# Loads of decay rows and pooling weights placed sooner, and branch gates with two buffers stored from ScalarE's queue

## The chip, the cores and the metric

One core of a Trainium2 chip runs the whole kernel. The metric is the device time in microseconds of one execution; the time given for a kernel is the median of its runs.

## The reference

One layer of a hybrid backbone over 512 latent tokens and 256 context tokens, model width 1024, all in fp32. It is a half-step SwiGLU feed-forward (inner width 2816), then token mixing, then a second half-step feed-forward and a final norm, all modulated by a condition (adaLN). The change lies in the mixing, of which this is the core:

```python
px = ux @ w_mix_in
pc = uc @ w_mix_in[:, :AB_END]
lat_in = gdn_inputs(px[..., :AB_END], conv_w, a_log, dt_bias)   # q, k, v, beta, g
ctx_in = gdn_inputs(pc[..., :AB_END], conv_w, a_log, dt_bias)
ox, oc = bidir_gdn(lat_in, ctx_in)
mix_x = merge_branches(px, pool_grid(px[..., GATE_END:POOL_END]), ox, ...)
x = x + mx[5] * mix_x
```

`gdn_inputs` makes q, k, v of 8 heads by a short convolution, and from four small columns per head a step size beta and a decay g. `bidir_gdn` runs a gated delta rule over chunks in both directions; it needs the running sums of g (`cum`) and the factors exp(cum_i - cum_j) of each chunk. `pool_grid` takes window means minus the token in 4 groups of 128 channels, and a linear map `pool_w` (128 x 128 in each group) follows. `merge_branches` computes `sigmoid(gate_pool) * (y_pool @ w_pool_proj) + sigmoid(gate_gdn) * (y_gdn @ w_gdn_proj)` and projects it with `w_mix_out`.

## The kernel before

Every product of two fp32 matrices is made of three matmuls: each operand is cast to fp32r (the high half, by ScalarE) and the rest is subtracted (the low half, by VectorE or GpSimd). `split_act` (lines 187 to 189) does this for an activation; `weights` (107 to 112) loads a slice of a weight matrix into the tile stg by SP's queue and makes whi and wlo of it; `job` (122 to 134) runs the matmuls at line 132.

The order of the instructions on an engine is not the order of the program text. A planner goes over the traced program and places an instruction on its engine when by its plan the inputs are there and the output tile has room; of several that could go, the earlier traced goes first. On the chip each engine, and each queue of transfers, then runs its list in that order. Tiles live in pools, and a pool lies on the bytes of pools that were closed before it; with a number of buffers (`bufs`) the tiles of one tag share so many homes. `tc.keep_in_program_order(i)` pins an instruction on its engine's list behind the instruction of that engine that was traced just ahead of it; it adds order and no wait.

Around the change the program does this:

- Decay stage (pool gp, lines 625 to 685). From the small columns come beta (639), nega (609), a sigmoid (650), Ln (652), g (660), the running sums by matmuls with the triangular matrices tri (loaded at 629, used at 665), and cumd, the sums of all heads as rows, stored to DRAM at 685. `head(0)` follows: the projections and convolutions of the first head's k, q and v.
- Pooling stage (pool pb, lines 688 to 731). pw (pool_w) is loaded at 693 and split. Twice, a half of the input weights, ws (1024 x 256, 1 MB, loaded at 700), is cast into wh and wl and multiplied at line 708 with the tokens. Then four groups of window sums, the product with pw, and the store of y into y_dram (731). `head(1)` follows.
- Heads (pool mp, from line 734, which begins with the small loads eye at 740 and first at 742). Each head has three generators. `front(h)` turns k and q by TensorE, copies k to kt on ScalarE (765), and prepares norms. `invert(h)` loads two tiles crow of 384 KB at 808 (the head's row sums of one direction, the same on all partitions; tag row, three buffers), makes of them arg (Abs on ScalarE, six times for each, 817; one Exp, 819), and inverts the chunk matrices. `scan(h)` is the recurrence over the chunks. `gate(h)` makes the head's output gate.
- Branch gates (`branch_gates`, 1028 to 1036): 16 jobs of 128 columns, each copied from PSUM to the tile bgate on ScalarE (1032; one buffer) and stored by SP's queue to bg_dram (1033).

The order of these parts is written out by hand: the loop over k runs scan(k), invert(k+1) and front(k+2) interleaved, then a later head, a gate, and so many branch gates as SHARE says for this k.

```python
    ORDER = "sfifsisiissiis"
    SHARE = (3, 2, 0, 0, 0, 0, 0, 0, 6, 5)
    for k in range(-2, H):
        stages = {c: g(i) for c, g, i in (("s", scan, k), ("f", front, k + 2), ("i", invert, k + 1)) if 0 <= i < H}
```

- Merge (pools mg and yp). The pooled rows y_dram come back into yg (tag yg, two buffers, loaded at 1078), and are split into yphi and yplo; then for each of 8 column blocks the gate is loaded, its sigmoid taken (1084), and `job` multiplies with w_pool_proj. The heads' outputs, yg_dram, pass through the same tag yg (1089), and gates and products with w_gdn_proj follow (1095 to 1100).

Of the kernel before, what the change touches and what calls it, by code (L numbers as in the profile page):

```python
# [8 lines left out]
F32 = mybir.dt.float32  # L9
F32R = mybir.dt.float32r  # L10
AF = mybir.ActivationFunctionType
ALU = mybir.AluOpType
# [5 lines left out]
KT = 8  # L18
LAT = 512
# [22 lines left out]
def layer_kernel(ctx, tc, a, out):  # L42
    nc = tc.nc
    act, dve, pool, pe, sp = nc.scalar, nc.vector, nc.gpsimd, nc.tensor, nc.sync
# [142 lines left out]
    def split_act(src, hi, lo):  # L187
        act.copy(out=hi, in_=src)  # L188
        dve.tensor_tensor(out=lo, in0=src, in1=hi, op=ALU.subtract)  # L189
# [193 lines left out]
    for k in range(KT):  # L383
        for p in BOTH:
            o, m = PARTS[p]
# [5 lines left out]
    with tc.tile_pool(name="pl", bufs=1, reuse_waits="tile") as pl:  # L391
# [5 lines left out]
        t = {}  # L397
# [3 lines left out]
        for n in range(KT + AHEAD):  # L401
            if n < KT:
                k = PAIRED[n]
# [185 lines left out]
    def head(h):  # L589

        for c0, tl, parts, store, tag, bufs in ((D, 8, BOTH, kf, "kf", 4), (0, 0, ONLY, qf, "qf", 4), (2 * D, 16, BOTH, vf, "vf", 2)):
            store[h] = pj.tile([128, T if len(parts) == 2 else LAT], F32, tag=tag, name=tag, bufs=bufs)
            if h == 0 and c0 == D:
                conv_silu(None, tl, parts, store[h], res_k)
            else:
                conv_silu(weights(w_mix, 0, KT, c0 + 128 * h, EH), tl + h, parts, store[h])
# [25 lines left out]
    bwst = sm.tile([128, 6, 8, 2], F32, name="bwst")  # L622
    ncumc = sm.tile([128, 96], F32, name="ncumc")
    etot = sm.tile([128, 96], F32, name="etot")
    with tc.tile_pool(name="gp", bufs=1, reuse_waits="tile") as gp:
        cumc = gp.tile([128, 96], F32, name="cumc")
        wst = gp.tile([128, 96], F32, name="wst")
# [60 lines left out]
    with tc.tile_pool(name="pb", bufs=1, reuse_waits="tile") as pb:  # L688

        phi = pb.tile([128, 4, 512], F32R, name="phi")  # L690
        plo = pb.tile([128, 4, 512], F32R, name="plo")
        pw = pb.tile([128, 4, 128], F32, name="pw")
        sp.dma_start(out=pw, in_=a["pool_w"].rearrange("(g p) m -> p g m", p=128))
        pwh = pb.tile([128, 4, 128], F32R, name="pwh")
        pwl = pb.tile([128, 4, 128], F32R, name="pwl")
        split_act(pw, pwh, pwl)
        for g2 in range(2):
            wh = pb.tile([128, KT, 256], F32R, tag="wh", name="wh", bufs=1)
            ws = pb.tile([128, KT, 256], F32, tag="ws", name="ws", bufs=2)
            sp.dma_start(out=ws, in_=w_mix[:, 4128 + 256 * g2:4384 + 256 * g2].rearrange("(k p) m -> p k m", p=128))  # L700
            wl = pb.tile([128, KT, 256], F32R, tag="wl", name="wl", bufs=1)
            split_act(ws, wh, wl)
            for t in range(4):
                r = bank("a")
                n = 0
                for k in range(KT):
                    for hh, ww in ((hhi, wh), (hlo, wh), (hhi, wl)):
                        pe.matmul(r[:, :256], lhsT=hh[:, k, t * 128:(t + 1) * 128], rhs=ww[:, k],  # L708
                                  start=n == 0, stop=n == 3 * KT - 1)
                        n += 1  # L710
                split_act(r[:, :256], phi[:, t, g2 * 256:g2 * 256 + 256], plo[:, t, g2 * 256:g2 * 256 + 256])
        for g in range(4):
# [16 lines left out]
            y = pb.tile([128, LAT], F32, tag="df", name="df", bufs=2)  # L729
            act.activation(out=y, in_=pr["lat"], func=AF.Copy, scale=vec[:, 0, R_PS + g:R_PS + g + 1])  # L730
            sp.dma_start(out=y_dram[g], in_=y)
    head(1)
    mp_cm = tc.tile_pool(name="mp", bufs=1, reuse_waits="tile")
    mp = mp_cm.__enter__()
# [8 lines left out]
    powers = mp.tile([128, 10], F32, name="powers")  # L743
    pool.memset(powers[:, 0:6], 0.5)
    pool.memset(powers[:, 6:10], -0.5)
    st = {}

    def g4(shape, name):
        return mp.tile(shape, F32, tag="g4", name=name, bufs=3)
# [6 lines left out]

    def front(h):

        kt = mp.tile([128, 6, 128], F32, tag="kt", name="kt", bufs=3)
        ss = mp.tile([128, 10], F32, tag="ss", name="ss", bufs=2)  # L760
        for c0, n in ((0, 4), (4, 2)):
# [32 lines left out]
        for c0, n in ((0, 4), (4, 2)):  # L794
            b = bank("a")
            for c in range(n):
                pe.transpose(b[:, c * 128:(c + 1) * 128], vf[h][:, (c0 + c) * 128:(c0 + c + 1) * 128], ident)
            dve.tensor_tensor(out=vt[:, c0:c0 + n], in0=b[:, :n * 128].rearrange("p (c x) -> p c x", x=128),
                              in1=bc(rr[:, c0:c0 + n].unsqueeze(2), [128, n, 128]), op=ALU.mult)
        st[h] = [kt, vt, rr, bs, nbs, w2]  # L800

    def invert(h):

        bs, nbs = st[h][3:5]
        crow = []
        for d in range(2):
            t = mp.tile([128, 6, 128], F32, tag="row", name="crow", bufs=3)
            sp.dma_start(out=t, in_=cum_rows[d, h].partition_broadcast(128))
            crow.append(t)

        L = mp.tile([128, 12, 128], F32, tag="L", name="L", bufs=2)
        aqk = mp.tile([128, 8, 128], F32, tag="aqk", name="aqk", bufs=2)
# [213 lines left out]
    def branch_gates():  # L1026
        jobs = []
        for m in range(2 * KT):
            def one(m=m):
                r = job(weights(w_mix, 0, KT, 4640 + 128 * m, EG), u_hi, u_lo, range(KT), ONLY)  # L1030
                t = mp.tile([128, LAT], F32, tag="bgate", name="bgate", bufs=1)
                act.copy(out=t, in_=r["lat"])
                sp.dma_start(out=bg_dram[m], in_=t)
            jobs.append(one)
        return jobs

# [29 lines left out]
    def m2(name, bufs=2):  # L1066
        return mg.tile([128, LAT], F32, tag=name, name=name, bufs=bufs)

    zhi, zlo = hhi[:, :, 0:LAT], hlo[:, :, 0:LAT]
    with tc.tile_pool(name="yp", bufs=1, reuse_waits="tile") as yp:  # L1070
# [3 lines left out]
        yplo = yp.tile([128, 4, LAT], F32R, name="yplo")  # L1074
        pooled = yp.tile([128, KT, LAT], F32, name="pooled")
        for g in range(4):
            t = m2("yg", 2)
            sp.dma_start(out=t, in_=y_dram[g])
            split_act(t, yphi[:, g], yplo[:, g])
        for m in range(0, KT, 2):  # L1080
            for e in range(2):
                gp_ = m2("gp")
# [2 lines left out]
                y = job(weights(a["w_pool_proj"], 0, 4, 128 * (m + e)), lambda k: yphi[:, k], lambda k: yplo[:, k], range(4), ONLY)["lat"]  # L1085
                dve.tensor_tensor(out=pooled[:, m + e], in0=gp_, in1=y, op=ALU.mult)
        for h in range(H):
            t = m2("yg", 2)
            sp.dma_start(out=t, in_=yg_dram[h])
            split_act(t, yghi[:, h], yglo[:, h])  # L1090
        sp.dma_start(out=xl, in_=x_dram)
# [176 lines left out]
```

## Time and profile before

| what | value |
|---|---|
| median of 3 runs | 1752.39 us |
| lowest and highest run | 1749.08 and 1753.36 us |
| the profiled execution, own time | 1756.71 us |
| the profiled execution, span | 1755.0 us |
| mean granted TensorE clock, share of full speed | 0.982 |
| TensorE busy | 1653.5 us, 94% of the span |
| ScalarE busy | 842.6 us, 48% |

The span runs from the first to the last instruction that the profiler recorded; the own time is the device time of that same execution. PE is TensorE's matmuls, PEld its weight loads, DVE VectorE, ACT ScalarE, POOL GpSimd, SP the engine whose queue issues nearly all transfers (SPq). In a wait, the tile or line behind the arrow is what ended the idle time. The granted clock is a share of full speed.

### The profile page before, as it was taken

How to read it: one execution, taken by the hardware profiler on the slowest of the kernel's cores; microseconds unless marked ns; L12 is line 12 of the kernel's file. 1: busy time of each engine (PE TensorE's matmuls, PEld its weight loads, DVE VectorE, ACT ScalarE, POOL GpSimd, SP SyncE). 2: the span in 40 equal slices, each digit the busy share in tenths (PEclk: the TensorE clock that was granted, in tenths of full speed). 3: DMA queues.
4: the chain of work that ended last, by engine and by line, in shares of the span. 5: the costliest groups of instructions: out<-in, count | busy, mean ns of one | idle time of the engine just before them, and what ended most of it. 6: DMA issues, size and time to landing. Idle time of an engine off the chain costs nothing.

```text
span 1755.0 us, 31315 instructions
## 1 busy us (share of the span) xinstructions
PE 1653.5 (94%) x12220; PEld 1423.9 (81%) x12220; DVE 1119.0 (64%) x2254; ACT 842.6 (48%) x1851; POOL 390.8 (22%) x493
## 2 busy tenths in 40 slices
PE   6899999999999999889999999999998999999996
PEld 4889898989999778777878788787786788888885
DVE  5778888798888886375678767774555533333333
ACT  5443343434444364667677767665443322222233
POOL 2243444444454121123323331100000000000000
PEclk9999999999999999989999999999999999999998
DMA  9355536361221325532112212224654232333321
GB/s 273 112 155 151 156 96 182 103 189 65 78 67 56 108 82 187 138 100 67 44 52 65 60 45 53 56 61 154 214 158 116 69 98 88 94 96 96 93 64 48
DMA packets 282696, 183.82 MB, mean 105 GB/s; under 512 B 7008, under 2 KB 269877, under 8 KB 282421
## 3 DMA queue, kind: packets, MB, share of 16 engines
q1 hardware_dynamic: 282112, 181.65, 35.6%
q8 instruction: 96, 1.57, 0.4%
q14 instruction: 51, 0.42, 0.1%
q10 hardware_dynamic: 437, 0.18, 0.1%
HBM read 170.22 MB, written 11.58 MB: 104 GB/s over the span
## 4 chain that ended last, share of the span: by engine, by line
PE 71%; DVE 14%; ACT 5%; DMA 5%; POOL 2%; issue 2%; SPq 0%; ACTq 0%; POOLq 0%; DVEq 0%
PE b L132 22%; PE b L345 9%; PE a L132 6%; PE g L132 6%; PE a L345 5%; PE g L345 5%; DVE cv L583 2%; PE b L279 2%; PE a L279 1%; PE g L279 1%; PE a L708 1%; ACT din L848 1%; DVE wlo L120 1%; DMA bg_dram<-bgate 1%; PE b L150 1%
## 5 line engine op out<-in xcount | busy, mean ns | idle before, releaser
L188 ACT CAST fhi<-fst 128x512 fp32r<-128x512 f32 (+1 forms) x136 | 77.7, 605 | 249.6 <-PE b L132 85.6
L132 PE MATMUL b<-hhi,whi 128*128 128x512 f32 (+1 forms) x528 | 187.6, 384 | 0.0
L132 PE MATMUL b<-hlo,whi 128*128 128x512 f32 (+1 forms) x528 | 187.5, 383 | 0.0
L132 PE MATMUL b<-hhi,wlo 128*128 128x512 f32 (+1 forms) x528 | 186.9, 384 | 0.0
L179 POOL TENSOR_TENSOR rs<-rs,mhalf 128x4 f32<-128x4 f32 (+2 forms) x13 | 13.6, 1045 | 665.3 <-DVE rs L177 649.7
L189 DVE TENSOR_TENSOR flo<-fst,fhi 128x512 fp32r<-128x512 f32 (+1 forms) x136 | 87.3, 671 | 92.6 <-ACT fhi L188 92.4
L119 ACT CAST whi<-stg 128x512 fp32r<-128x512 f32 x146 | 89.4, 620 | 91.6 <-PE b L132 59.9
L119 ACT CAST whi<-qst 128x512 fp32r<-128x512 f32 (+1 forms) x160 | 81.6, 512 | 106.5 <-PE b L345 43.2
L119 ACT CAST whi<-qs 128x512 fp32r<-128x512 f32 (+1 forms) x120 | 59.5, 512 | 115.2 <-POOL qs L309 76.2
L583 DVE SCALAR_TENSOR_TENSOR cv<-raw,vec,cv 128x772 f32<-128x772 f32 (+1 forms) x96 | 101.6, 1058 | 11.6 <-ACT cv L581 8.3
L120 DVE TENSOR_TENSOR wlo<-qst,whi 128x512 fp32r<-128x512 f32 (+1 forms) x160 | 100.7, 639 | 10.1 <-ACT whi L119 10.0
L132 PEld LDWEIGHTS b<-hlo,whi 128*128 128x128 f32 x528 | 94.0, 190 | 14.8
L132 PEld LDWEIGHTS b<-hhi,whi 128*128 128x128 f32 x528 | 94.0, 190 | 14.8
L132 PEld LDWEIGHTS b<-hhi,wlo 128*128 128x128 f32 x528 | 93.3, 190 | 14.8
L308 POOL TENSOR_TENSOR qs<-qst 128x512 f32<-128x512 f32 (+1 forms) x40 | 46.4, 1161 | 247.2 <-DMA qst<-in_ffn_w_in_dram 76.6
L120 POOL TENSOR_TENSOR wlo<-stg,whi 128x512 fp32r<-128x512 f32 x46 | 65.4, 1430 | 90.6 <-ACT whi L119 70.6
L120 DVE TENSOR_TENSOR wlo<-stg,whi 128x512 fp32r<-128x512 f32 x100 | 68.2, 686 | 22.1 <-ACT whi L119 20.2
L188 ACT CAST ahi<-q 128x384 fp32r<-128x384 f32 x74 | 37.5, 512 | 75.4 <-DVE q L257 35.6
L120 DVE TENSOR_TENSOR wlo<-qs,whi 128x512 fp32r<-128x512 f32 (+1 forms) x80 | 49.0, 613 | 32.6 <-ACT whi L119 32.6
L132 PE MATMUL b<-xlo,fhi 128*128 128x512 f32 x160 | 63.4, 396 | 0.0
L132 PE MATMUL b<-xhi,flo 128*128 128x512 f32 x160 | 63.4, 396 | 0.0
L132 PE MATMUL b<-xhi,fhi 128*128 128x512 f32 x160 | 63.4, 396 | 0.0
(512 smaller groups left out, 4909.8 us busy)
## 6 DMA issues: line engine op xcount, KB each, us to landing
stg<-in_w_ada_dram SPq DMA_DIRECT2D x56, 512.0 KB, 4.0
stg<-in_w_mix_in_dram SPq DMA_DIRECT2D x49, 512.0 KB, 3.7
fst<-in_ffn_w_in_dram SPq DMA_DIRECT2D x44, 512.0 KB, 3.6
qst<-in_ffn_w_in_dram SPq DMA_DIRECT2D x40, 512.0 KB, 3.4
qst<-in_ffn_w_out_dram SPq DMA_DIRECT2D x40, 256.0 KB, 2.6
adx<-in_w_ada_dram SPq DMA_DIRECT2D x16, 512.0 KB, 6.4
fst<-in_ffn_w_out_dram SPq DMA_DIRECT2D x16, 512.0 KB, 3.9
crow<-cumd SPq DMA_DIRECT2D x16, 384.0 KB, 7.8
```

Source lines behind the costliest of these rows:

```text
L119: (first.copy if first is act else first.tensor_copy)(out=hi[:, :n], in_=w)
L120: second.tensor_tensor(out=lo[:, :n], in0=w, in1=hi[:, :n], op=ALU.subtract)
L132: pe.matmul(res[p][:, :m], lhsT=ww(i), rhs=hh(k)[:, o:o + m], start=(i == 0 and j == 0), stop=(i == n - 1 and j == 2))
L150: pe.matmul(b[32 * j:32 * j + 32, e * 128:(e + 1) * 128], lhsT=sc[:, k, :], rhs=stg[:, k, :], start=(i == 0), stop=(i == 1))
L188: act.copy(out=hi, in_=src)
L189: dve.tensor_tensor(out=lo, in0=src, in1=hi, op=ALU.subtract)
L279: pe.matmul(x, lhsT=ww(k), rhs=rhs(j, part, k), start=n + e == 0, stop=n + e == len(ks) + 1)
L308: pool.tensor_tensor(out=s1, in0=a21, in1=a22, op=ALU.add)
L345: pe.matmul(o, lhsT=ww[:, k], rhs=rhs(j, part, k), start=first and k + i == 0, stop=k + i == nh + 1, skip_group_check=not first)
L583: dve.scalar_tensor_tensor(out=cv[:, :n], in0=raw[:, t:t + n], scalar=tap[t], in1=cv[:, :n], op0=ALU.mult, op1=ALU.add)
L708: pe.matmul(r[:, :256], lhsT=hh[:, k, t * 128:(t + 1) * 128], rhs=ww[:, k], start=n == 0, stop=n == 3 * KT - 1)
L848: act.copy(out=din[o:o + 32, :, 0:12].rearrange("p f u -> p u f"), in_=L[o:o + 32, :, o:o + 32])
```

## The change

Four edits. A pool pw is opened ahead of the decay stage's pool; it holds both ws (homes of their own), pw, pwh and pwl, and their loads and the split of pw are traced there. The two crow loads move from `invert(h)` to the start of `front(h)`, with four buffers in place of three. bgate gets two buffers, and its store is issued by ScalarE's queue. In the merge the tag yg gets four buffers, and the casts yphi are pinned in program order; yplo isn't.

```diff
--- before.py
+++ after.py
@@ -622,6 +622,16 @@
     bwst = sm.tile([128, 6, 8, 2], F32, name="bwst")
     ncumc = sm.tile([128, 96], F32, name="ncumc")
     etot = sm.tile([128, 96], F32, name="etot")
+    pw_cm = tc.tile_pool(name="pw", bufs=1, reuse_waits="tile")
+    pwp = pw_cm.__enter__()
+    pool_w = [pwp.tile([128, KT, 256], F32, tag="ws", name="ws", bufs=2) for _ in range(2)]
+    for g2 in range(2):
+        sp.dma_start(out=pool_w[g2], in_=w_mix[:, 4128 + 256 * g2:4384 + 256 * g2].rearrange("(k p) m -> p k m", p=128))
+    pw = pwp.tile([128, 4, 128], F32, name="pw")
+    sp.dma_start(out=pw, in_=a["pool_w"].rearrange("(g p) m -> p g m", p=128))
+    pwh = pwp.tile([128, 4, 128], F32R, name="pwh")
+    pwl = pwp.tile([128, 4, 128], F32R, name="pwl")
+    split_act(pw, pwh, pwl)
     with tc.tile_pool(name="gp", bufs=1, reuse_waits="tile") as gp:
         cumc = gp.tile([128, 96], F32, name="cumc")
         wst = gp.tile([128, 96], F32, name="wst")
@@ -689,15 +699,9 @@
 
         phi = pb.tile([128, 4, 512], F32R, name="phi")
         plo = pb.tile([128, 4, 512], F32R, name="plo")
-        pw = pb.tile([128, 4, 128], F32, name="pw")
-        sp.dma_start(out=pw, in_=a["pool_w"].rearrange("(g p) m -> p g m", p=128))
-        pwh = pb.tile([128, 4, 128], F32R, name="pwh")
-        pwl = pb.tile([128, 4, 128], F32R, name="pwl")
-        split_act(pw, pwh, pwl)
         for g2 in range(2):
             wh = pb.tile([128, KT, 256], F32R, tag="wh", name="wh", bufs=1)
-            ws = pb.tile([128, KT, 256], F32, tag="ws", name="ws", bufs=2)
-            sp.dma_start(out=ws, in_=w_mix[:, 4128 + 256 * g2:4384 + 256 * g2].rearrange("(k p) m -> p k m", p=128))
+            ws = pool_w[g2]
             wl = pb.tile([128, KT, 256], F32R, tag="wl", name="wl", bufs=1)
             split_act(ws, wh, wl)
             for t in range(4):
@@ -729,6 +733,7 @@
             y = pb.tile([128, LAT], F32, tag="df", name="df", bufs=2)
             act.activation(out=y, in_=pr["lat"], func=AF.Copy, scale=vec[:, 0, R_PS + g:R_PS + g + 1])
             sp.dma_start(out=y_dram[g], in_=y)
+    pw_cm.__exit__(None, None, None)
     head(1)
     mp_cm = tc.tile_pool(name="mp", bufs=1, reuse_waits="tile")
     mp = mp_cm.__enter__()
@@ -743,7 +748,7 @@
     powers = mp.tile([128, 10], F32, name="powers")
     pool.memset(powers[:, 0:6], 0.5)
     pool.memset(powers[:, 6:10], -0.5)
-    st = {}
+    st, rows_of = {}, {}
 
     def g4(shape, name):
         return mp.tile(shape, F32, tag="g4", name=name, bufs=3)
@@ -756,6 +761,11 @@
 
     def front(h):
 
+        crow = []
+        for d in range(2):
+            t = mp.tile([128, 6, 128], F32, tag="row", name="crow", bufs=4)
+            sp.dma_start(out=t, in_=cum_rows[d, h].partition_broadcast(128))
+            crow.append(t)
         kt = mp.tile([128, 6, 128], F32, tag="kt", name="kt", bufs=3)
         ss = mp.tile([128, 10], F32, tag="ss", name="ss", bufs=2)
         for c0, n in ((0, 4), (4, 2)):
@@ -798,15 +808,12 @@
             dve.tensor_tensor(out=vt[:, c0:c0 + n], in0=b[:, :n * 128].rearrange("p (c x) -> p c x", x=128),
                               in1=bc(rr[:, c0:c0 + n].unsqueeze(2), [128, n, 128]), op=ALU.mult)
         st[h] = [kt, vt, rr, bs, nbs, w2]
+        rows_of[h] = crow
 
     def invert(h):
 
         bs, nbs = st[h][3:5]
-        crow = []
-        for d in range(2):
-            t = mp.tile([128, 6, 128], F32, tag="row", name="crow", bufs=3)
-            sp.dma_start(out=t, in_=cum_rows[d, h].partition_broadcast(128))
-            crow.append(t)
+        crow = rows_of.pop(h)
 
         L = mp.tile([128, 12, 128], F32, tag="L", name="L", bufs=2)
         aqk = mp.tile([128, 8, 128], F32, tag="aqk", name="aqk", bufs=2)
@@ -1028,9 +1035,9 @@
         for m in range(2 * KT):
             def one(m=m):
                 r = job(weights(w_mix, 0, KT, 4640 + 128 * m, EG), u_hi, u_lo, range(KT), ONLY)
-                t = mp.tile([128, LAT], F32, tag="bgate", name="bgate", bufs=1)
+                t = mp.tile([128, LAT], F32, tag="bgate", name="bgate", bufs=2)
                 act.copy(out=t, in_=r["lat"])
-                sp.dma_start(out=bg_dram[m], in_=t)
+                act.dma_start(out=bg_dram[m], in_=t)
             jobs.append(one)
         return jobs
 
@@ -1074,9 +1081,10 @@
         yplo = yp.tile([128, 4, LAT], F32R, name="yplo")
         pooled = yp.tile([128, KT, LAT], F32, name="pooled")
         for g in range(4):
-            t = m2("yg", 2)
+            t = m2("yg", 4)
             sp.dma_start(out=t, in_=y_dram[g])
-            split_act(t, yphi[:, g], yplo[:, g])
+            tc.keep_in_program_order(act.copy(out=yphi[:, g], in_=t))
+            dve.tensor_tensor(out=yplo[:, g], in0=t, in1=yphi[:, g], op=ALU.subtract)
         for m in range(0, KT, 2):
             for e in range(2):
                 gp_ = m2("gp")
@@ -1085,7 +1093,7 @@
                 y = job(weights(a["w_pool_proj"], 0, 4, 128 * (m + e)), lambda k: yphi[:, k], lambda k: yplo[:, k], range(4), ONLY)["lat"]
                 dve.tensor_tensor(out=pooled[:, m + e], in0=gp_, in1=y, op=ALU.mult)
         for h in range(H):
-            t = m2("yg", 2)
+            t = m2("yg", 4)
             sp.dma_start(out=t, in_=yg_dram[h])
             split_act(t, yghi[:, h], yglo[:, h])
         sp.dma_start(out=xl, in_=x_dram)
```

## Rows read from the trace of the kernel before

**Rows 1.** The page's busy time, share of the span and instructions of each engine.
```profile
PE 1653.5 (94%) x12220; PEld 1423.9 (81%) x12220; DVE 1119.0 (64%) x2254; ACT 842.6 (48%) x1851; POOL 390.8 (22%) x493
```
**Rows 2.** TensorE's waits: what for, us in total, times, longest us.
```profile
PE a L771 <- ACT kt L765: 9.0, 1, 9.0
...
PE a L881 <- DVE tr L872: 4.7, 6, 2.4
...
PE a L708 <- ACT wh L188: 3.3, 1, 3.3
PE b L132 <- ACT yphi L188: 3.3, 1, 3.3
```
**Rows 3.** Windows; us, busy (instructions) of each engine, TensorE's granted clock, DMA share, GB/s.
```profile
641.00:669.28 28.28, 28.28 (x155) 23.73 (x153) 22.14 (x49) 21.48 (x35) 11.47 (x14) 1.00 0.46 132
672.62:677.34 4.72, 4.72 (x19) 4.11 (x20) 4.42 (x4) 2.99 (x7) 0.10 (x1) 0.64 1.05 395
783.15:786.57 3.42, 3.42 (x23) 2.28 (x15) 3.42 (x5) 1.11 (x2) 0.00 (x0) 0.50 0.02 5
979.00:982.00 3.00, 1.00 (x8) 0.69 (x7) 2.59 (x3) 1.01 (x3) 1.55 (x4) 1.00 0.14 30
1238.26:1243.95 5.69, 5.68 (x12) 3.71 (x13) 2.30 (x5) 1.69 (x3) 0.00 (x0) 0.50 0.42 138
```
**Rows 4.** The chain that ended last, 655 to 690; start us, us, what.
```profile
654.97 0.35 PE a L665 x3
...
663.12 7.52 DMA ws<-in_w_mix_in_dram
```
**Rows 5.** Timeline of SP's queue, 636 to 666; start, us, engine, line, operation.
```profile
640.38 0.43 SPq L629 DMA_DIRECT2D tri<-in_consts_dram  x1
644.49 13.76 SPq L110 DMA_DIRECT2D stg<-in_w_mix_in_dram  x2
658.30 0.57 SPq L685 DMA_DIRECT2D cumd<-rt  x1
```
**Rows 6.** Timeline of ScalarE, 640 to 675; in brackets idle before and releaser.
```profile
670.67 1.90 ACT L188 CAST wh<-ws 128x2048 fp32r<-128x2048 f32 x1 [2.83 <-DMA ws<-in_w_mix_in_dram]
```
**Rows 7.** Timeline of ScalarE, 730 to 751.
```profile
735.81 1.86 ACT L817 ACTIVATE arg<-crow,ncumc 128x128 f32<-128x128 f32 x6 [4.03 <-DMA crow<-cumd]
740.68 0.40 ACT L817 ACTIVATE arg<-crow,ncumc 128x128 f32<-128x128 f32 x1 [3.01 <-DMA crow<-cumd]
741.46 0.58 ACT L1032 COPY bgate<-b 128x512 f32<-128x512 f32 x1 [0.37 <-DMA bg_dram<-bgate]
...
748.15 0.58 ACT L1032 COPY bgate<-b 128x512 f32<-128x512 f32 x1 [1.34 <-DMA bg_dram<-bgate]
748.63 0.87 ACT L765 COPY kt<-a 128x512 f32<-128x512 f32 x2
```
**Rows 8.** The same chain, 728 to 752, and the gate's stores as one tile.
```profile
729.95 11.41 DMA bg_dram<-bgate
...
L1033 SPq DMA_DIRECT2D bg_dram<-bgate x16: 319/338/1206, 729.9 to 1236.1; - x16
```
**Rows 9.** Timeline of SP's queue, 720 to 736.
```profile
726.31 0.53 SPq L740 DMA_DIRECT2D eye<-in_consts_dram  x1
...
727.37 1.01 SPq L808 DMA_DIRECT2D crow<-cumd  x2
```
**Rows 10.** Timeline of ScalarE, 1228 to 1239.
```profile
1235.51 0.58 ACT L1032 COPY bgate<-b 128x512 f32<-128x512 f32 x1
...
1237.59 1.13 ACT L188 CAST yphi<-yg 128x512 fp32r<-128x512 f32 x2
```
**Rows 11.** ScalarE's waits, 785 to 1215, the largest.
```profile
ACT whi L119 <- PE b L132: 35.0, 19, 2.9
```
**Rows 12.** The waits of SP's queue, the one for bgate.
```profile
SPq L1033 <- ACT bgate L1032: 78.0, 13, 11.4
```
**Rows 13.** Waits of TensorE's weight loads, the one at line 665.
```profile
PEld a L665 <- DVE g L660: 0.2, 1, 0.2
```

## The prediction

> **What bounds the kernel.** The busy shares come first: TensorE works for 1653.5 us, 94% of the span [rows 1]. So two things can be won: its idle time, and time at the lower of its two clock levels (0.50 of full speed, 1.2 GHz). Next I read the list of what TensorE waited for. Four of its waits lie where the diff works: 9.0 us at line 771 on ScalarE's copy kt, 3.3 at line 708 on the cast wh, 3.3 at line 132 on the cast yphi, and one of 2.4 at line 881, some 30 us behind the first [rows 2]. Then the windows around them: the stretch behind the idle time at line 708 has a mean clock of 0.64, the one behind yphi 0.50 for 5.69 us, the one behind line 881's 0.50 [rows 3]. Last, the timelines of ScalarE and of SP's queue say what was late in each. The profiled execution took 1756.71 us, 4.32 above the median of 1752.39; the sum is made against it and carried to the median by subtraction.
>
> **Stall A, the pooling weights.** TensorE worked without a gap up to 669.28 [rows 3] and then stood 3.3 us. The chain of waits names the load of ws: issued at 663.12, it took 7.52 us [rows 4]. It waited for its place on the queue, not for data: behind cumd's store at 658.30, the last transfer of the decay stage, while weight loads that the program traces later went out at 644.49 [rows 5]. So I read it as waiting for the decay stage's space. In homes opened ahead of that stage, ws and pw go out where tri does, at about 640.4 [rows 5], and if they take as long as now they are there by 649, twenty us early; in front of wh TensorE has 28.28 us of work without a gap [rows 3], which covers it. ScalarE stood idle 2.83 us before the cast wh [rows 6], so nothing else is late there. Gain: 3.3 us of idle time and the half speed behind it, where 4.72 us at 0.64 did 4.72 x 0.64 = 3.0 us of work, so that 1.7 are lost. **A = -5.0**, with bounds 0 (wh no sooner) and -5.0. What the move costs: tri, now behind 2.25 MB, lands up to 7.5 us later than after its issue at 640.38, and line 665 first reads it at 654.97 [rows 4]: 0. The cast of pw is the same cast on the same engine, only sooner: 0, unless it waits (second rival).
>
> **Stall B, the first head.** Reading ScalarE's queue backwards from kt at 748.63: a bgate copy that had waited 1.34 for its store, five arg operations, a bgate copy that had waited 0.37, the seventh arg, 3.01 behind the second row load, and the first six, 4.03 behind the first [rows 7]. The store went out on SP's queue at 729.95, behind two row loads, and took 11.41 us [rows 8]. The row loads went out at 727.37, a microsecond behind eye, the first load of the same pool [rows 9]: the place of these too is that of a stage just opened. Traced in front(), a few instructions sooner, the first pair stays where it is, and with it the 4.03 and 3.01. What goes: with two bgate buffers no copy waits for the store ahead of it (0.37 + 1.34), and the first of the two copies, 0.58, is made before the rows arrive, while ScalarE idles. Against that stands one store's issue, 0.34 [rows 8]: 1.71 + 0.58 - 0.34. **B = -2.0.** The later 2.4 us at line 881 wait for VectorE's chain [rows 2], so nothing more is won there. The upper bound is the whole stall, -9.0, if the rows come in time. The lower is +4.9: the second head's rows, no longer held by SP's wait for a buffer, go out ahead of the second head's weights, and one row load behind another took 740.68 - 735.81 = 4.9 us [rows 7]. I take the value next to the waits that the row shows.
>
> At this place a rule bears on the sum. The gate's store leaves SP's row of transfers for ScalarE's, and no execution here has both rows loaded at once. By the Trainium skill ("DMA: Bandwidth & Descriptors", section "Queues, rings and completion order") a DMA engine takes turns between the rows that have work, so the store would get ahead of the row loads in place of standing behind them. By that rule the second row lands up to 0.7 us later (the store landed at 729.95 + 11.41 = 741.36, that row just ahead of the seventh arg at 740.68), B would be -1.3 and the sum -8.3. The trace neither bears it out nor excludes it.
>
> **Stall C, the merge.** TensorE waited for yphi up to 1238.26. Ahead of yphi, ScalarE made the last bgate at 1235.51, a sigmoid and a weight cast, and began yphi at 1237.59 [rows 10]. Pinned, yphi stands behind the last gate's store and ahead of casts that are ready later: of the 2.08 us between the two starts the copy's 0.59 stay, 1.5 go, and 0.34 of issue come in, so 1.1 are won. The 5.69 us at 0.50 behind it [rows 3] lost 2.85. After an idle stretch of some 2.1 the clock may fall or not: 979 to 982 holds an idle stretch of 2.0 and stays at 1.00, the 2.4 at line 881 were followed by 0.50 [rows 2, 3]. I take half, 1.4. **C = -2.5**, with bounds +1 (pinned casts of 0.6 hold back a sigmoid or a weight cast) and -6.1 (all of it). The two further yg buffers let the third and fourth loads go out before the casts: 0, since TensorE's wait was for the first.
>
> **Sixteen stores on ScalarE's queue.** An issue took 338 ns in the median, 1206 at most [rows 8]: 16 x 0.34 = 5.4 us on an engine that is 48% busy [rows 1]. Between 785 and 1215 ScalarE stood 35.0 us waiting for TensorE before its weight casts alone [rows 11], and most issues fall into such waits. I take a tenth, **+0.5**, with bounds 0 and 16 x 1.2 = 19.2. A store waits for the copy just ahead of it on its own engine, so nothing new is queued behind a foreign event. SP's queue loses 78.0 us of waits for bgate [rows 12], ahead of weight loads; TensorE's list has no wait on those: 0.
>
> **Sum:** -5.0 - 2.0 - 2.5 + 0.5 = -9.0: 1747.7 for the profiled execution, **1743.4** against the median. What a measurement of this kernel can tell from no change is about 0.3%, 5.3 us: 1747.1 to 1757.7 counts as the same.
>
> **The rivals.**
> 1. *Stall B goes whole.* For it: seven of its nine us hang on two row loads. Against: their place follows eye's, which the change doesn't move. -5.0 - 9.0 - 2.5 + 0.5 = -16.0: 1736.4. Chance 0.22.
> 2. *The cast of pw becomes a wait in the decay stage.* pw is now queued behind 2 MB of ws. If its cast stands on ScalarE ahead of that stage's sigmoid, at 643 or 644, it holds the queue until 649, some 5 us; line 665's weight load had waited only 0.2 us for that stage's last product, so it has no slack [rows 13]. TensorE then stands 5.0 + 0.6 for the cast, and 1.7 of half speed follow as behind stall A: +7.3, less the 9.0, so 1750.7. Against: ready matmuls of the first head can stand ahead of line 665. Chance 0.10.
> 3. *Slower: the stores break into the scans.* The scan is a recurrence through TensorE, VectorE and ScalarE. If a store holds the next instruction of ScalarE there, 16 stores count in full. This decides from 9.5 / 16 = 0.6 us each; at the longest issue, 1.2, it costs 19.2: -9.5 + 19.2 = +9.7, so 1762. For it: ScalarE's copies are links of the recurrence. Against: the median of 0.34. Chance 0.16.
> 4. *Stall A stays*, since the cast wh gets no better place: -4.0, so 1748.4. Chance 0.06.
> 5. *The second head's rows delay its weights*: +4.9 in place of -2.0, so 1750.3. Chance 0.06.
>
> **How the numbers follow.** My own case has 0.40, of it 0.36 below 1747.1 and 0.04 above. Faster: 0.36 + 0.22 = 0.58. Within the bound: 0.04 + 0.10 + 0.06 + 0.06 = 0.26. Slower: 0.16. The range reaches down past the first rival with its C at the bound (1736.4 - 3.6 = 1732.8), to 1731, and up to 1756, past rivals 2, 4 and 5; the third lies outside.
>
> **What would show it.** A: ws issued before 645 and no wait for wh. B: kt copied some 2 us sooner, no bgate waiting for a store, the first row load still behind eye. C: yphi right behind the last store. Stores: their durations on ScalarE's queue, and no longer waits in the scans. It would be wrong if a wait for pw stood ahead of line 665, if kt came as late as before, or if TensorE's idle time between 785 and 1215 grew.

## The result and the profile after

The changed kernel takes 1768.2 us (median of 6 runs, 1761.07 to 1774.07) where the kernel before takes 1752.2: a ratio of 1.0093, with an interval of 1.0068 to 1.0118. It is 16 us slower, 12 us above the upper end of the range. The profiled execution took 1774.07, with a span of 1772.3; it is the longest of the six, so its trace shows more of the loss than the median has.

The busy shares of the page of the changed kernel, which answer to [rows 1]:

```profile
PE 1669.2 (94%) x12220; PEld 1436.5 (81%) x12220; DVE 1115.0 (63%) x2254; ACT 846.6 (48%) x1853; POOL 393.1 (22%) x493
```

ScalarE is busy 4.0 us more. What grew is TensorE's busy time, 15.7 us for the same 12220 matmuls, while its idle time (span less busy time) went only from 101.5 to 103.1 us. The windows below show that these are matmuls at the lower clock. TensorE's waits in the changed kernel, answering to [rows 2] (what for, us in total, times, longest us):

```profile
PE g L1021 <- ACT ot L1018: 8.4, 7, 1.3
...
PE a L888 <- DVE tr L879: 7.0, 8, 4.6
...
PE b L132 <- ACT whi L119: 3.9, 1, 3.9
PE a L781 <- ACT kt L775: 3.7, 1, 3.7
PE b L132 <- ACT yphi L1086: 3.3, 1, 3.3
...
PE a L712 <- DVE wl L189: 1.9, 1, 1.9
```

The lines have moved: 781 is line 771 of before, 888 is 881, 712 is 708, 1021 is 1014. No stall is simply gone. The 9.0 us at kt became 3.9 for a weight cast and 3.7 for kt; the 3.3 at wh became 1.9 for its other half, wl; the 3.3 for yphi is the same; line 888 waits 4.6 where 881 waited 2.4. And the top entry is new: at the end of seven of the eight heads TensorE waits for ot, the head's output that it is to transpose, five times for 1.3 us. Before, it did so once, for 1.0.

Windows say where the clock went. First the middle of the heads' loop in the kernel before, then the same in the changed kernel, with one head's end in detail (columns as in [rows 3]):

```profile
785.00:1130.00 345.00, 328.69 (x3947) 276.06 (x3946) 249.98 (x593) 250.55 (x664) 100.77 (x179) 1.00 0.22 55
```

```profile
785.00:1130.00 345.00, 326.99 (x3686) 274.30 (x3685) 234.79 (x559) 244.37 (x646) 99.06 (x175) 0.95 0.20 52
...
844.86:846.14 1.28, 0.00 (x1) 0.00 (x1) 0.00 (x0) 0.46 (x2) 0.74 (x3) 1.00 0.05 13
846.14:850.00 3.86, 3.86 (x21) 3.08 (x22) 1.77 (x3) 3.40 (x9) 0.00 (x0) 0.62 0.11 43
850.00:860.75 10.75, 10.75 (x55) 8.67 (x55) 2.69 (x3) 4.17 (x9) 2.57 (x4) 0.50 0.02 9
```

In 345 us TensorE's idle time grew by 1.7 us only (328.69 to 326.99 busy), but the mean clock fell from 1.00 to 0.95: 345 x 0.05 = 17 us of work lost, as much as the 17.4 us between the two profiled executions. The last three rows show how: a wait of 1.28 us for ot, and behind it 0.62 and then 0.50 for almost 15 us.

What stands around that wait differs between the kernels. The timeline of TensorE, first before, at the ends of two heads in a row, then after:

```profile
910.57 0.19 PE L906 MATMUL a<-U,x 32*32 32x32 f32 x1
910.69 0.66 PE L1014 MATMUL g<-ident,ot 128*128 128x128 f32 x4
...
968.51 0.40 PE L132 MATMUL b<-hhi,whi 128*128 128x512 f32 x1
968.75 0.27 PE L1014 MATMUL g<-ident,ot 128*128 128x128 f32 x1
```

```profile
844.65 0.19 PE L912 MATMUL a<-x,U 32*32 32x32 f32 x1
844.67 0.19 PE L913 MATMUL a<-U,x 32*32 32x32 f32 x1
846.14 0.92 PE L1021 MATMUL g<-ident,ot 128*128 128x128 f32 x3 [1.28 <-ACT ot L1018]
```

Before, two forms take turns: at one head's end the four transposes of ot stand directly behind the inversion's 32 x 32 matmuls (lines 905 and 906), at the next, matmuls of a weight job lie between and among them. In both, ot is ready when its turn comes. After, the transposes stand directly behind the 32 x 32 matmuls at the end of every head up to 1100, and TensorE, which runs its list in order, waits. In the instruction lists of the two programs this repeats: before, the order comes back every two heads; after, every head. The planner wrote another list, though no line of the scan's or the inversion's arithmetic was changed. The two are called the paired order and the single order below.

SP's and ScalarE's timelines of the changed kernel, for the steps of the prediction:

```profile
635.11 1.18 SPq L629 DMA_DIRECT2D ws<-in_w_mix_in_dram  x2
636.35 4.04 SPq L631 DMA_DIRECT2D pw<-in_pool_w_dram  x1
...
711.60 7.23 SPq L767 DMA_DIRECT2D crow<-cumd  x4
718.92 10.46 SPq L110 DMA_DIRECT2D stg<-in_w_mix_in_dram  x2
```

```profile
719.39 0.40 ACT L824 ACTIVATE arg<-crow,ncumc 128x128 f32<-128x128 f32 x1 [0.53 <-DMA crow<-cumd]
...
723.51 1.86 ACT L824 ACTIVATE arg<-crow,ncumc 128x128 f32<-128x128 f32 x6 [0.17 <-DMA crow<-cumd]
735.38 0.62 ACT L119 CAST whi<-stg 128x512 fp32r<-128x512 f32 x1 [10.01 <-DMA stg<-in_w_mix_in_dram]
...
1253.31 2.18 ACT L1086 CAST yphi<-yg 128x512 fp32r<-128x512 f32 x4 [0.98 <-DMA bg_dram<-bgate]
```

ws went out before 645, as forecast. The first head's rows came in time, which was not forecast: ScalarE waited 0.53 and 0.17 us for them, where it had waited 4.03 and 3.01 [rows 7]. But the rows of two heads went out together, ahead of the next weights, and ScalarE stood 10.01 us for those weights with kt behind them in its list. And yphi waited for the last gate's store to land.

### The profile page after: what moved, and what is told of

Its sections match the earlier page's. It is cut to its first block, busy times and chain, and to the rows that moved or that the text cites. A ratio compares the mean times of both kernels' runs of the same rounds, so it can differ in the third digit from the quotient of the medians.

```text
span 1772.3 us, 31301 instructions
## 1 busy us (share of the span) xinstructions
PE 1669.2 (94%) x12220; PEld 1436.5 (81%) x12220; DVE 1115.0 (63%) x2254; ACT 846.6 (48%) x1853; POOL 393.1 (22%) x493
## 4 chain that ended last, share of the span: by engine, by line
PE 72%; DVE 15%; DMA 4%; ACT 4%; issue 2%; POOL 2%; SPq 0%; POOLq 0%; ACTq 0%; DVEq 0%
PE b L132 22%; PE b L345 9%; PE g L132 6%; PE a L132 6%; PE a L345 5%; PE g L345 5%; DVE cv L583 2%; PE b L279 2%; PE a L279 1%; DMA stg<-in_w_mix_in_dram 1%; PE g L279 1%; PE a L712 1%; ACT din L855 1%; PE b L150 1%; DVE wlo L120 1%
## 5 line engine op out<-in xcount | busy, mean ns | idle before, releaser
L132 PE MATMUL b<-hhi,whi 128*128 128x512 f32 (+1 forms) x528 | 191.4, 394 | 3.9 <-ACT whi L119 3.9
L132 PEld LDWEIGHTS b<-hlo,whi 128*128 128x128 f32 x528 | 96.4, 196 | 15.4
```

The source lines that it names most:

```text
L132: pe.matmul(res[p][:, :m], lhsT=ww(i), rhs=hh(k)[:, o:o + m], start=(i == 0 and j == 0), stop=(i == n - 1 and j == 2))
```

## The experiments

Twelve kernels ran, each with its own runs of the kernel before beside it. Ratios are to those, with 95% intervals.

| run | edits | median us | before us | ratio |
|---|---|---|---|---|
| e1 | store on ScalarE's queue | 1764.62 | 1754.35 | 1.0054 [1.0033, 1.0074] |
| e2 | store on ScalarE's queue, two gate buffers | 1756.51 | 1754.35 | 1.0010 [0.9995, 1.0025] |
| e3 | all but the store's move | 1760.19 | 1754.35 | 1.0034 [1.0020, 1.0048] |
| e4 | all but the pooling weights | 1758.90 | 1754.35 | 1.0026 [1.0012, 1.0040] |
| e5 | pooling weights | 1755.27 | 1752.06 | 1.0014 [1.0000, 1.0028] |
| e6 | all, one gate made later | 1763.67 | 1752.06 | 1.0054 [1.0031, 1.0077] |
| e7 | merge casts | 1752.01 | 1752.06 | 1.0000 [0.9982, 1.0017] |
| e8 | rows | 1758.17 | 1752.06 | 1.0031 [1.0014, 1.0047] |
| e9 | e1 without the head's norm in ot | 1746.41 | 1754.70 | 0.9951 [0.9936, 0.9966] |
| e10 | pooling weights, two gate buffers | 1748.67 | 1754.70 | 0.9963 [0.9948, 0.9978] |
| e11 | e10, first head's rows and wl earlier | 1751.50 | 1754.70 | 0.9988 [0.9976, 1.0000] |
| e12 | two gate buffers | 1752.52 | 1752.57 | 0.9996 [0.9981, 1.0012] |

### The store's move, alone and with two buffers

The theory from the two traces was that the list's order costs; the rivals were the stores themselves and the row loads ahead of the weights. The planner's lists tell the first two apart: with the store's move alone the heads get the single order, with two buffers added they keep the paired one in the middle of the loop, and both have all 16 stores on ScalarE's queue.

```diff
-                sp.dma_start(out=bg_dram[m], in_=t)
+                act.dma_start(out=bg_dram[m], in_=t)
```

> Only the store of the branch gates moves to ScalarE's queue; one buffer, and all else as before. Order theory: with this edit alone the instruction lists of the heads settle into the order that the changed kernel has (the 48 pairs of short matmuls of line 912 and 913 together, and right behind them the four transposes of ot), so TensorE waits 1.2 to 1.3 us for ot in most heads and the clock falls to 0.50 several times between 785 and 1230: 12 to 22 us slower than before, 1764 to 1774. Store theory (each store costs ScalarE its issue and nothing else): 16 x 0.34 = 5.4 us at most, so 1752 to 1758. Row theory (the four row loads ahead of the weights are what costs): no change, 1749 to 1755.

```diff
-                t = mp.tile([128, LAT], F32, tag="bgate", name="bgate", bufs=1)
+                t = mp.tile([128, LAT], F32, tag="bgate", name="bgate", bufs=2)
...
-                sp.dma_start(out=bg_dram[m], in_=t)
+                act.dma_start(out=bg_dram[m], in_=t)
```

> The branch gates' edit whole (two buffers, store on ScalarE's queue), all else as before. Here the heads' lists keep the order of before in the middle of the loop. Order theory: no fall of the clock between 785 and 1150, so 1746 to 1756, though all 16 stores are on ScalarE's queue. Store theory: the same as the run with the store alone, within 3 us. Row theory: no change.

The first lost 0.54%, 9.5 us (12 to 22 were forecast), the second 0.10%, in an interval that holds no change. In the first, TensorE's waits between 785 and 1130 have the new entry, and the window has 4.1 us more idle time than before and a mean clock of 0.98:

```profile
PE g L1014 <- ACT ot L1011: 6.4, 5, 1.3
```

```profile
785.00:1130.00 345.00, 324.62 (x3885) 271.96 (x3886) 242.32 (x572) 247.80 (x653) 101.05 (x179) 0.98 0.21 54
```

In the second no wait for ot is in that list, and the stores stand on ScalarE's queue as one tile row shows (duration least, median, most):

```profile
L1033 ACTq DMA_DIRECT2D bg_dram<-bgate x16: 326/327/402, 729.1 to 1235.6; - x16
```

The store theory had the two runs within 3 us of each other, and they are 8 apart, so it is out. The stores cost what the sum said, little; the order that their move brings about costs the rest.

### The whole change without one part

```diff
-                act.dma_start(out=bg_dram[m], in_=t)
+                sp.dma_start(out=bg_dram[m], in_=t)
```

> The whole change, but the gates' store stays on SP's queue. The heads' lists have the order of before. Order theory: faster than the changed kernel by 15 to 25 us, 1743 to 1753. Store theory: faster than the changed kernel by at most 5.4, so 1763 or more. Row theory: the four row loads still stand ahead of the weights, so slower than before by 3 to 8 us: 1755 to 1760.

The other run leaves out the new pool pw and keeps all else.

> The whole change, but the pooling weights stay where they were. The heads' lists have the order of before in the middle of the loop. Order theory: 1745 to 1755, although the stores are on ScalarE's queue and the rows go out early. Store theory: as the changed kernel or slower, 1766 to 1774, since only a gain is taken out. Row theory: 1755 to 1760.

Both have the paired order in the middle of the loop, and both are faster than the changed kernel, by 0.59% and 0.67% as ratios to before, with intervals that don't meet its own. But both are slower than before, and clear of it: 1.0034 and 1.0026, where the order theory had them at 1743 to 1753 and 1745 to 1755 us. So the order is not the whole loss. TensorE's waits in the run with the store on SP's queue show what else there is:

```profile
PE b L132 <- ACT yphi L1086: 5.4, 1, 5.4
...
PE a L781 <- ACT kt L775: 3.8, 1, 3.8
PE b L132 <- ACT whi L119: 3.6, 1, 3.6
```

From 640 to 785 TensorE is even idle for less time, 12.7 us where it was 15.4 before. But the one stall at kt is now two, and the mean clock of that stretch is 0.93 where it was 0.96, which is some 145 x 0.03 = 4.4 us. At yphi 2.1 us of idle time come on top. The row theory, which named the four row loads ahead of the weights, had forecast 3 to 8 us of loss here and came out at 5.9.

### Each other part alone

The pooling weights' pool alone (the first, second and fourth hunk of the change):

> Only the pooling weights' and pw's move. The heads' lists keep the order of before. By the sum of the prediction: 5.0 us faster, with no wait at line 708. Rival, from the profile of the whole change without the store's move (1.8 us of wait for wl, and still 3.4 us at 0.50 behind it): the cast's other half is late next, and only 1.5 us are won, 1751 to 1754 where before is at 1754.

It was slower by 0.14%, an interval that touches 1; neither the 5.0 us of the sum nor the rival's 1.5 was won. Its waits, and ScalarE's row ahead of kt:

```profile
PE a L776 <- ACT kt L770: 7.4, 1, 7.4
...
PE a L712 <- DVE wl L189: 1.8, 1, 1.8
```

```profile
746.26 0.58 ACT L1037 COPY bgate<-b 128x512 f32<-128x512 f32 x1 [6.23 <-DMA bg_dram<-bgate]
```

wl is VectorE's half of the split; it stands in VectorE's list behind the decay stage and the convolution. So the edit wins 1.6 us of TensorE's idle time there. It also brings the first head's rows sooner: ScalarE waited 1.34 and 0.31 us for them, for 4.03 and 3.01 before. The first head makes little of that, since a gate's copy then waited 6.23 us for a store, and kt behind it.

The merge casts alone (the four yg buffers and the pin):

> Only the four yg buffers and the pinned casts. By the sum of the prediction: 2.5 us faster. Rival, from the two profiles that have this edit (5.4 and 3.5 us of wait for yphi, where before has 3.3): the casts come no sooner, since they stay behind a weight cast, and 0 to 4 us are lost: 1754 to 1758.

Ratio 1.0000. The wait for yphi is one microsecond shorter, near the 1.1 of the sum. The interval is 3 us to either side, so the forecast gain of 2.5 can't be told from none:

```profile
PE b L132 <- ACT yphi L1079: 2.3, 1, 2.3
```

The rows alone:

> Only the row loads' move to front, with four buffers. By the sum of the prediction 0 us, since the first pair stays where it is. Rival (four row loads go out together, ahead of the second head's weights): kt is no sooner, a weight cast waits for its load for more than 2 us, and 1 to 5 us are lost: 1755 to 1759. Third: the rows of the later heads come sooner and the first stall shrinks, 2 to 9 us won.

Slower by 0.31%, 5.4 us: the rival's size by another way. The weight cast is not late here; TensorE waits 11.5 us for kt where it waited 9.0 before, since the gate's copy ahead of kt waits 4.18 for a store that left SP's queue behind two more row loads and a weight load:

```profile
PE a L776 <- ACT kt L770: 11.5, 1, 11.5
```

```profile
726.35 6.50 SPq L762 DMA_DIRECT2D crow<-cumd  x2
732.94 4.75 SPq L110 DMA_DIRECT2D stg<-in_w_mix_in_dram  x1
737.79 3.37 SPq L1035 DMA_DIRECT2D bg_dram<-bgate  x1
```

```profile
746.70 0.58 ACT L1034 COPY bgate<-b 128x512 f32<-128x512 f32 x1 [4.18 <-DMA bg_dram<-bgate]
747.18 0.87 ACT L770 COPY kt<-a 128x512 f32<-128x512 f32 x2
```

The second gate buffer alone:

```diff
-                t = mp.tile([128, LAT], F32, tag="bgate", name="bgate", bufs=1)
+                t = mp.tile([128, LAT], F32, tag="bgate", name="bgate", bufs=2)
```

> Only the second gate buffer; the store stays on SP's queue, the lists of TensorE, VectorE and GpSimd are those of before, and ScalarE's differs in the gates' copies alone. By the term of the sum: the two waits of 0.37 and 1.34 us and one copy go ahead of kt, so the wait at kt is 6 to 8 us and the kernel 0 to 3 us faster, 1751 to 1755 where before is at 1754. If the two edits of the run with weights and two buffers (6 us faster) simply add up, and the weights alone lose 2 to 3 us, this must win 8 to 9: 1744 to 1747. Then the first is wrong.

The wait at kt fell from 9.0 to 6.4, as the term of the sum had it, and the time didn't change measurably (0.9996):

```profile
PE a L771 <- ACT kt L765: 6.4, 1, 6.4
```

### The order taken back in the whole change

A list can be nudged. With one branch gate made in the last round of heads in place of the second, the whole change gets the paired order.

```diff
-    SHARE = (3, 2, 0, 0, 0, 0, 0, 0, 6, 5)
+    SHARE = (3, 1, 0, 0, 0, 0, 0, 0, 6, 6)
```

> The whole change, with one number more: one of the two branch gates of the second round of heads is made in the last round (SHARE 3, 1, ..., 6, 6). With that the heads' lists have the order of before again (46 pairs of short matmuls apart from the transposes of ot in six of eight heads); stores, rows, weights and pins are those of the changed kernel. Order theory: no wait for ot above 1.1 us before 1130 and at most one fall of the clock between 785 and 1130, 8 to 14 us faster than the changed kernel: 1755 to 1760. If the loss came from the edits themselves and not from the order: 1764 to 1772.

1.0054 against the changed kernel's 1.0093: some 0.39%, 7 us, come back (4.5 by the medians, 1763.67 for 1768.2). That is less than the expected 8 to 14; the median lies between the two theories' ranges, just below the lower end of the rival's, and the intervals meet, so the time of this run alone doesn't decide. The clock in the middle of the loop is 1.00 again, as the order theory had it. Behind 1130 it is 0.94: there TensorE waits twice for ot, 1.5 us each, and the clock falls both times, so that 7 us is rather a lower figure for the order:

```profile
785.00:1130.00 345.00, 329.44 (x4044) 277.41 (x4044) 251.14 (x596) 253.00 (x674) 97.13 (x177) 1.00 0.22 54
1130.00:1262.00 132.00, 122.73 (x1036) 98.66 (x1026) 67.84 (x158) 71.15 (x159) 8.04 (x15) 0.94 0.42 132
```

The parts alone lose 0.14% (weights), 0.31% (rows), 0.10% (gates with both edits) and 0.00% (merge): 0.55% together, which is this run's 0.54%. That fits a plain sum in the paired order, with the single order on top. The intervals of the four are wide enough that the agreement to 0.01% is luck.

### The wait taken out of the single order

Is it the order's row of short matmuls that lets the clock fall, or the wait behind it? In the kernel with the store's move alone, this run scales ot by the factor of q only, which is ready long before; it leaves out the norm of each head's output. The list stays in the single order up to 1100.

```diff
-            act.activation(out=ot[:, c], in_=ot[:, c], func=AF.Copy, scale=r[:, c:c + 1])
+            act.activation(out=ot[:, c], in_=ot[:, c], func=AF.Copy, scale=rr[:, 6 + c:7 + c])
```

> The kernel with the store's move alone, whose heads' lists have the slow order, and in it the scaling of ot takes the factor of q in place of the head's norm: the norm of each head's output is left out, so that ScalarE doesn't wait for GpSimd's pow ahead of TensorE's transposes of ot. The 48 pairs of short matmuls still stand together in front of the transposes. If the wait behind the short matmuls is what costs: no wait for ot of over 1 us before 1100 and at most one fall of the clock between 785 and 1130, 6 to 12 us faster than the run with the store alone: 1750 to 1757. If the row of short matmuls itself lets the clock fall: the falls stay, and only the waits themselves go, five of 1.27: 1757 to 1763.

It took 0.9951 of before, and about 1% less than the same kernel with the wait, more than either theory had. Five waits of 1.3 us are 6.4 us; with them the falls of the clock went. The edit takes other waits away too: over the whole span TensorE is idle 97.8 us, for 107.1 in e1. So the time is no price of the order, but the clock in the middle of the loop answers the question:

```profile
785.00:1130.00 345.00, 330.31 (x4111) 278.93 (x4110) 253.34 (x600) 256.61 (x682) 100.84 (x176) 1.00 0.22 56
```

Without its wait the single order even comes out ahead of before (with a norm's wait less on ScalarE's list, though, so that this is no fair race). The row of short matmuls alone doesn't lower the clock here; it takes the wait behind it. The kernel before says the same: every other head there has the transposes right behind such a row, without a wait (910.57 and 910.69 above), and its clock is 1.00 from 785 to 1130.

### Two versions that should be faster

The weights and the second buffer, the store on SP's queue, rows and merge untouched:

> The pooling weights' move and two gate buffers, the store on SP's queue; rows and merge as before. The heads' lists have the order of before. In the run with the weights alone kt still waited 6.2 us for a bgate copy, which waited for its store behind two row loads. With the second buffer that wait goes: 4 to 7 us less idle time at kt than there, 1746 to 1751. If something else is late next (the weight cast, the Exp): 1752 to 1756.

0.9963, 6.5 us faster than before and some 1.3% faster than the changed kernel. Of the wait for kt 0.8 us are left. Its waits at the places of the change:

```profile
PE a L712 <- DVE wl L189: 1.4, 1, 1.4
...
PE a L776 <- ACT kt L770: 0.8, 1, 0.8
```

Alone neither part wins (1.0014 and 0.9996): with the weights alone kt hangs on the gate's buffer, with the buffer alone on the row loads, which there still came 4 us late. It is the weights' move that brings these sooner: in the five kernels that have it and load the rows in the heads' pool, ScalarE's wait for the first row is 0.5 to 1.5 us, in the eight without it 4.0 to 5.1. The last version also gives the first head's rows a home below the heads' pool, loaded right behind cumd, and traces the first split of the weights ahead of the decay stage:

```diff
+    wh0 = pwp.tile([128, KT, 256], F32R, tag="wh", name="wh", bufs=1)
+    wl0 = pwp.tile([128, KT, 256], F32R, tag="wl", name="wl", bufs=1)
+    split_act(pool_w[0], wh0, wl0)
...
+    rows_of = {0: rows(0)}
     y_dram = dr.tile([4, 128, LAT], F32, name="y_dram")
     head(0)
```

> As the run before it, and two things more: the first head's rows have a home of their own below the heads' pool and are loaded right behind cumd (two buffers for the later heads), and the first half of the pooling weights is split into wh and wl ahead of the decay stage in the program, so that VectorE's list has wl early. The heads' lists have the order of before. If the two stalls were rows and wl: no wait at the pooling matmuls, under 3 us at kt, 6 to 14 us faster than before: 1738 to 1748. If wl on VectorE or the loads delay the decay stage, as the prediction's second rival has it: a wait of over 2 us at the decay matmuls, and 1750 or more.

0.9988, slower than the version before it, where 6 to 14 us faster than before were forecast. The wait at kt is gone and the one for wl became 1.9 us for the low half of another operand, but a new stall stands between them: the row loads now precede the window tiles on SP's queue, ScalarE stood 12.06 us for a window tile, and the second half of the weights was cast behind it.

```profile
PE a L729 <- ACT wh L188: 8.0, 1, 8.0
```

```profile
677.41 1.90 ACT L739 CAST win<-wst 128x2048 fp32r<-128x2048 f32 x1 [12.06 <-DMA wst<-in_window_dram]
```

## Why the prediction was wrong

**The sum had no term for the order.** It took the lists of the heads' loop as given and asked only which waits go. The step that failed here is the one on the sixteen stores, "+0.5": its price and its cover fit what e2 measured, and what it left out is that their move makes the planner write another list for the heads. In the whole change the single order goes if either the store's move or the pooling weights' is taken out (e3, e4); with one gate buffer the store's move alone brings it (e1). The runs price it at 7 to 9.5 us (e6, e1), or 4.5 by e6's medians. In the changed kernel's trace nearly all of it is clock, in e1's about 4 us are idle time.

**The three gains failed as well, and that is the larger part.** From the forecast -9.0 to the measured +16 are 25 us, and the order has 7 to 9.5 of them. With the order taken back the whole change still lost 0.54%, 9.5 us, where the sum had 9.0 to win.

**The slower rival had the sign and nearly the size, and the wrong mechanism.** 1762 was forecast for stores that break into the scans; that it came near is luck. The stores cost nothing that can be measured, and of the sixteen only three lie between 780 and 1140. "If TensorE's idle time between 785 and 1215 grew" was the sign to look for; the idle time there grew by 2.0 us, and the clock fell.

**Stall A, -5.0.** ws was early, as forecast, and the cast wh with it. "Nothing else is late there" failed: wl was, by 1.8 us, because it stands in VectorE's list behind the decay stage, and the half speed came back behind that wait. The term is -1.6 in idle time and 0 in clock; alone the edit measured 1.0014, so that not even the 1.6 show.

**Stall B, -2.0.** The buffer's part was right: 2.6 us less at kt in e12, with 2.0 forecast. "The first pair stays where it is, and with it the 4.03 and 3.01" failed: the pair still stood right behind eye and first, but the edit of stall A, which the first rival's "against" took to leave eye alone, brought all of them sooner (0.53 and 0.17 us of waits in the changed kernel, 1.34 and 0.31 in e5). So the first rival's condition came true, and its 7 us were lost again to what was late next: the second pair goes out with the first, and the weights behind them came 10.01 us late. The fifth rival (chance 0.06, +4.9 for -2.0) names this. In e8 the rows alone lost 5.4, there by the store of a gate that was late.

**Stall C, -2.5.** The pin was to put yphi behind the last gate's store. It did, and yphi waited for that store to land: the store left at 1251.29 and yphi began at 1253.31, and TensorE's idle time is 3.3 us before and after. The wait doesn't need the pin. It stands in the run with the rows alone too, which has no pin and the store on SP's queue. And being behind a store on its own queue isn't enough: in e2 yphi, not pinned, follows such a store without it:

```profile
1237.29 1.14 ACT L188 CAST yphi<-yg 128x512 fp32r<-128x512 f32 x2 [1.01 <-DMA bg_dram<-bgate]
```

```profile
1235.60 0.33 ACTq L1033 DMA_DIRECT2D bg_dram<-bgate  x1
1235.96 1.14 ACT L188 CAST yphi<-yg 128x512 fp32r<-128x512 f32 x2 [0.40 <-ACT bgate L1032]
```

The four kernels that show it (the changed one, e4, e6, e8) all have the four row buffers. That yphi's home lies on bgate's bytes once the pool is larger is a reading that no run tests, and no run has the pin and that store without the row buffers. Alone the edit measured 1.0000, which excludes neither 0 nor the forecast 2.5.

**The second rival**, a wait for pw in the decay stage, didn't come: ScalarE waited 0.52 us for pw in the changed kernel, and TensorE 0.5 for the decay product.

**What stays open.** In the changed kernel the clock fell behind four of the five waits of 1.3 us between 840 and 1100, in e1 behind three of the five, and in the kernel before it fell behind none of its waits of up to 2.0 us in that stretch. (In e10 it did, once: behind an idle stretch of 2.0 us at 970.) e9 shows that the falls go when the waits go; what tells a wait that lowers the clock from one that doesn't was not settled. Why the weights alone, at 1.6 us less idle time, aren't faster is open as well. Nor was it settled why the planner's order changes to the single form with the store's move, and back with a second buffer when the weights stay put; the lists show that it does.

## What to carry to other kernels

Where a planner writes the lists, compare the lists of both programs over the whole loop before adding up waits: an edit at the loop's start can change the order of every round. A load made earlier is won only if the next thing in line (the other half of the split, the buffer behind it, the weights that share the queue) is ready too, so edits that are worthless alone can be worth 6 us together, as in e10. And an edit to one stage can move the loads of the next, so a wait that the sum keeps is to be read again for each edit.

## What the runs showed of the hardware

A small wait can cost five times its length: 1.28 us of idle time at 844.86 was followed by 3.86 us at 0.62 and 10.75 at 0.50, some 7 us of work. Another of 1.27 us, at 969.5 in the same execution, was followed by none.

A store on another engine's queue landed no sooner than behind the row loads. In e1 the first gate's store left on ScalarE's queue at 728.22 while three row loads were under way on SP's, and the chain of waits has it landing 14.11 us later, where on SP's queue, behind two of them, it took 11.41 [rows 8]:

```profile
728.22 14.11 DMA bg_dram<-bgate
```

The row below is the window behind its issue (columns as in [rows 3]):

```profile
728.22:734.00 5.78, 5.78 (x28) 4.68 (x27) 1.02 (x2) 1.11 (x2) 4.32 (x3) 1.00 0.28 76
```

The prediction read the Trainium skill ("DMA: Bandwidth & Descriptors", section "Queues, rings and completion order") to say that the engines' turn-taking between rows would let the store go ahead. The measurement decides against that reading here. The transfers ahead didn't fill the DMA engines, which were busy 0.28 of that window; what held the store was not settled.
